# A hybrid encoder layer: the input projection of twelve of seventeen tiles in seven-product form, with the heads' data kept in DRAM and one triangular solve per group

## The chip, the cores and the metric

The kernel runs on one NeuronCore of a Trainium2 chip. The metric is the device time of one execution in microseconds (us). Engines are named as in the profile: PE (TensorE), DVE (VectorE), ACT (ScalarE), POOL (GpSimd), SP (the sync engine, which here only issues transfers).

## The reference

One layer runs over 2048 new prompt frames (16 tiles of 128 rows) and over eight running streams of 16 frames (one more tile, "the sample tile", number 16). Width is 1024, everything is float32.

```
h = rmsnorm(x, norm_mix_pre);  P = h @ w_in        # 1024 -> 3592 columns
q,k,v = silu(causal_dwconv4(P[:, :1536]));  q,k = l2norm per head (4 heads x 128)
beta = sigmoid(b);  g = -exp(a_log) * softplus(a + dt_bias)
S_t = exp(g_t) (I - beta_t k_t k_t^T) S_{t-1} + beta_t k_t v_t^T;  o_t = S_t^T q_t
o = rmsnorm_head(o) * silu(z);  y = B * causal_dwconv3(C * H)
x = x + rmsnorm(concat(o, y) @ w_o)
x = x + rmsnorm((silu(h2 @ w_gate) * (h2 @ w_up)) @ w_down),  h2 = rmsnorm(x)
```

The recurrence is computed tile by tile: a unit lower triangular 128 x 128 matrix per tile and head is inverted, and the state S passes from tile to tile. Outputs are y, the new states and the last rows of both convolutions.

## The kernel before

Every float32 product is split into a rounded part and a remainder (hi and lo, type fp32r) and made from three products: hi·hi, hi·lo, lo·hi. A split is a cast on ACT and a subtraction on DVE or POOL.

The kernel has four stages. The first is what the change touches:

- **First stage.** `GROUPS` holds six groups of three tiles (the last has two). For each group the loop in the body runs, in this order: `x_prep` (row norms, split of the transposed input into eight hi and eight lo tiles), `gate_prep`, `qkv_stage`, `pair_stage`, `level_stage`, `z_stage`, a `chunk_stage` or `sample_stage` for each tile, `sc_stage`.
- `project` (its products are recorded at L136, the helper `mm3`) makes one of 28 column blocks of 128: eight k-slices times three products, 128x128 against the group's 384 (or 256) columns, into one PSUM bank. The bank pool psd has three. `weights` splits a block the first time (L338 cast, L340 subtraction), writes the split form to DRAM (`wsplit`, L343), and later groups load 1 MB back from there (L332). Some blocks are split in every second group or in the last one as well.
- `conv_qkv` does the causal convolution: a copy out of PSUM (L379), a first multiply (L381), three taps (L367), SiLU (L390). Keys are transposed, scaled and transposed back; queries and values are transposed. Results stay in SBUF.
- `pair_stage` makes, for each tile, the matrices k·k and k·q with decay (L491, L492, L495, L496), sends the sixteen 32 x 32 diagonal blocks of each tile to DRAM, gathers them with one block on each partition, and solves all of the group's blocks at once: 31 steps of a product and a subtraction on DVE (L511, L513), 48 partitions for three tiles.
- `level_stage` brings the inverted blocks back and joins them to inverses of 64 and of 128 (L538 to L562); a POOL memset (L552) stands between two of its steps. `chunk_stage` advances the state (L592 to L609) and makes the output (L613 to L619); `out_stage` norms it and writes it to `mixd`.
- **Output projection** (`o_tile`, L758): one tile at a time, reading `mixd`, all 17.
- **Feed-forward, up** (L963) and **down** (L1122) use a seven-product scheme: a 2 x 2 block product is made from seven block products instead of eight, of sums of the weight blocks and of the input blocks, and recombined on ACT, DVE and POOL (L999 to L1014). Sums of the weights are L929 to L932, splits L938 and L939.

The order of instructions on each engine comes from a scheduler that runs through the program in order of a simulated time; earlier program text has the higher priority. Loads are issued by SP, most stores by ACT's queue, each queue in order.

## Time and profile before

| | us |
|---|---|
| runs shown, median (lowest to highest) | 2668.58 (2663.05 to 2671.18) |
| profiled execution, span | 2659.7 |
| PE / DVE / ACT / POOL busy | 2533.2 / 1717.3 / 971.8 / 939.5 |
| first stage, first to last projection product | 22.5 to 991 |
| output projection | 1010 to 1225 |
| feed-forward up | 1225 to 2167 |
| feed-forward down | 2167 to 2660 |

Of the profiled execution only the span is known, the time from its first to its last instruction. Busy times are those of instructions; issuing transfers and waiting on semaphores are not counted. PE's records are pipelined, so neighbouring products overlap in them: the pitch from start to start says what one costs.

### The profile page before, as it was taken

How to read it: one execution, taken by the hardware profiler on the slowest of the kernel's cores; microseconds unless marked ns; L12 is line 12 of the kernel's file. 1: busy time of each engine (PE TensorE's matmuls, PEld its weight loads, DVE VectorE, ACT ScalarE, POOL GpSimd, SP SyncE). 2: the span in 40 equal slices, each digit the busy share in tenths (PEclk: the TensorE clock that was granted, in tenths of full speed). 3: DMA queues.
4: the chain of work that ended last, by engine and by line, in shares of the span. 5: the costliest groups of instructions: out<-in, count | busy, mean ns of one | idle time of the engine just before them, and what ended most of it. 6: DMA issues, size and time to landing. Idle time of an engine off the chain costs nothing.

```text
span 2659.7 us, 42363 instructions
## 1 busy us (share of the span) xinstructions
PE 2533.2 (95%) x15129; PEld 2357.1 (89%) x15129; DVE 1717.3 (65%) x3403; ACT 971.8 (37%) x2337; POOL 939.5 (35%) x841
## 2 busy tenths in 40 slices
PE   7989899999999989999999999999899999999997
PEld 6889789989899987878999999999899987887776
DVE  7788567667575875676978863433633344677698
ACT  5535115142251524433434432222323335333343
POOL 2321001000010210224556654443544445555563
PEclk9999989999999998999999999999999999999999
DMA  6876576666657555667877777877888852443365
GB/s 206 293 255 243 166 245 216 226 225 239 214 207 248 177 182 173 230 214 250 309 261 271 265 259 250 282 247 240 286 287 278 276 169 87 129 123 119 126 217 176
DMA packets 322403, 589.46 MB, mean 222 GB/s; under 512 B 57116, under 2 KB 206304, under 8 KB 303376
## 3 DMA queue, kind: packets, MB, share of 16 engines
q1 hardware_dynamic: 193600, 510.01, 56.7%
q10 hardware_dynamic: 128592, 76.74, 9.5%
q8 instruction: 120, 1.97, 0.3%
q14 instruction: 91, 0.75, 0.1%
HBM read 424.60 MB, written 162.05 MB: 221 GB/s over the span
## 4 chain that ended last, share of the span: by engine, by line
PE 67%; DVE 13%; DMA 8%; issue 4%; ACT 3%; POOL 2%; SPq 1%; ACTq 1%; DVEq 0%; POOLq 0%
PE fbank L963 28%; PE dbank L136 16%; PE fbank L1122 10%; PE tbank L758 3%; PE dbank L758 3%; DMA w<-wsplit 2%; DMA wr<-in_w_in 1%; DVE acc L367 1%; DVE xl L894 1%; POOL dw L829 1%; DMA dr<-in_w_dn 1%; DVE xr L1137 1%; DVE acc L1081 1%; DVE acc L1136 1%; DMA xt<-in_x 1%
## 5 line engine op out<-in xcount | busy, mean ns | idle before, releaser
L963 PE MATMUL fbank<-xh,fw 128*128 128x384 f32 (+1 forms) x3696 | 904.2, 327 | 19.7 <-ACT m L999 12.1
L136 PE MATMUL dbank<-hi,w 128*128 128x384 f32 (+1 forms) x2688 | 691.9, 336 | 16.6 <-DMA w<-wsplit 9.7
L963 PEld LDWEIGHTS fbank<-xh,fw 128*128 128x128 f32 x3696 | 654.9, 189 | 23.4 <-ACT m L999 14.2
L963 PE MATMUL fbank<-xl,fw 128*128 128x384 f32 (+1 forms) x1848 | 604.2, 327 | 0.0
L136 PEld LDWEIGHTS dbank<-hi,w 128*128 128x128 f32 x2688 | 484.8, 193 | 22.8 <-POOL w L340 8.4
L1122 PE MATMUL fbank<-dw,as 128*128 128x512 f32 x1980 | 463.2, 395 | 14.3 <-ACT dw L827 5.0
L1122 PEld LDWEIGHTS fbank<-dw,as 128*128 128x128 f32 x1980 | 372.0, 189 | 105.2 <-DVE acc L1081 7.4
L136 PE MATMUL dbank<-lo,w 128*128 128x384 f32 (+1 forms) x1344 | 449.5, 335 | 0.0
L963 PEld LDWEIGHTS fbank<-xl,fw 128*128 128x128 f32 x1848 | 348.9, 189 | 0.0
L136 PEld LDWEIGHTS dbank<-lo,w 128*128 128x128 f32 x1344 | 259.0, 193 | 1.7 <-issue 0.8
L1106 POOL TENSOR_TENSOR as<-ar,as 128x256 fp32r<-128x256 f32 (+1 forms) x207 | 188.2, 918 | 171.8 <-ACT as L1103 170.4
L939 POOL TENSOR_TENSOR fw<-rg,fw 128x512 fp32r<-128x512 f32 x124 | 176.5, 1424 | 180.9 <-ACT fw L938 180.7
L1081 DVE TENSOR_TENSOR acc<-acc,fbank 128x512 f32<-128x512 f32 x248 | 166.6, 682 | 99.6 <-PE fbank L1122 79.6
L1103 ACT CAST as<-ar 128x256 fp32r<-128x256 f32 (+1 forms) x288 | 118.3, 427 | 181.8 <-PE fbank L1122 132.7
L340 POOL TENSOR_TENSOR w<-wr,w 128x512 fp32r<-128x512 f32 x49 | 78.3, 1599 | 223.6 <-ACT w L338 188.0
L938 ACT CAST fw<-rg 128x512 fp32r<-128x512 f32 x124 | 77.5, 625 | 185.1 <-PE fbank L963 147.9
L367 DVE SCALAR_TENSOR_TENSOR acc<-R,cw,acc 128x384 f32<-128x384 f32 (+1 forms) x216 | 131.0, 609 | 2.0
L1007 DVE TENSOR_TENSOR u<-m,fbank 128x384 f32<-128x384 f32 (+1 forms) x66 | 34.8, 528 | 143.3 <-PE fbank L963 130.4
L1008 POOL TENSOR_TENSOR m<-m,m 128x384 f32<-128x384 f32 (+1 forms) x66 | 69.4, 1051 | 159.5 <-ACT m L1001 119.0
L939 POOL TENSOR_TENSOR fw<-ru,fw 128x512 fp32r<-128x512 f32 x62 | 92.3, 1488 | 85.8 <-ACT fw L938 70.2
L1012 DVE TENSOR_TENSOR c<-u,fbank 128x384 f32<-128x384 f32 (+1 forms) x66 | 34.9, 528 | 127.8 <-PE fbank L963 127.6
L552 POOL MEMSET AU<- 32x128 f32 x16 | 3.2, 197 | 281.0 <-PE gbank L538 272.1
(322 smaller groups left out, 3807.2 us busy)
## 6 DMA issues: line engine op xcount, KB each, us to landing
w<-wsplit SPq DMA_DIRECT2D x119, 1024.0 KB, 6.0
fw<-fsplit SPq DMA_DIRECT2D x188, 512.0 KB, 4.7
fsplit<-fw SPq DMA_DIRECT2D x94, 512.0 KB, 4.1
partd<-pt ACTq DMA_DIRECT2D x88, 384.0 KB, 6.0
rg<-in_w_gu SPq DMA_DIRECT2D x62, 512.0 KB, 3.7
wsplit<-w SPq DMA_DIRECT2D x28, 1024.0 KB, 4.7
wr<-in_w_in SPq DMA_DIRECT2D x98, 256.0 KB, 4.4
ar<-partd SPq DMA_DIRECT2D x48, 384.0 KB, 3.3
```

Of the source, the lines that this page charges most:

```text
L136: T.matmul(ps, l, r, start=(i == 0), stop=(i == n - 1))
L340: e.tensor_tensor(out=wl[:, c], in0=wr, in1=wh[:, c].bitcast(F32), op=ALU.subtract)
L367: V.scalar_tensor_tensor(acc, raw(d), w[:, d:d + 1], acc, op0=ALU.mult, op1=ALU.add)
L758: T.matmul(pss[n], m_[:, j, :], w_[k][:, n * 512:(n + 1) * 512], start=(k == 0 and ci == 0), stop=(k == KD - 1 and ci == 2))
L938: A.copy(w[:, 0], v)
L939: e.tensor_tensor(out=w[:, 1], in0=v, in1=w[:, 0].bitcast(F32), op=ALU.subtract)
L963: T.matmul(ps, w_[:, c], b_[k][:, :hw], start=(first and k == 0 and ci == 0), stop=(k == KH - 1 and ci == 2), skip_group_check=not first)
L1008: G.tensor_tensor(out=s7, in0=s7, in1=s5, op=ALU.add)
L1081: V.tensor_add(dst, dst, ps)
L1103: ins = A.copy(a[:, 0, :n], v)
L1106: e.tensor_tensor(out=a[:, 1, :n], in0=v, in1=a[:, 0, :n].bitcast(F32), op=ALU.subtract)
L1122: T.matmul(ps, a[:, x_, q * P:(q + 1) * P], w[:, y_], start=(start and q == 0 and ci == 0), stop=(q == c - 1 and ci == 2), skip_group_chec ...
```

## The change

The tiles are grouped anew and the groups are taken in pairs, "super-groups" of five, six and six tiles:

```
-GROUPS = [[0, 1, 16], [2, 3, 4], [5, 6, 7], [8, 9, 10], [11, 12, 13], [14, 15]]
+GROUPS = [[0, 1, 16], [2, 3], [4, 5, 6], [7, 8, 9], [10, 11, 12], [13, 14, 15]]
+SUPER = [[0, 1], [2, 3], [4, 5]]
-NPD, NPT, NPG = 3, 2, 2
+NPD, NPT, NPG = 4, 2, 2
+NX, NX0, NW, NWR, NST, NACC = 56, 32, 8, 4, 2, 3
```

The 28 column blocks are taken in 14 pairs, in the order z, k, q, v, z, then the short convolution's blocks. The first super-group projects as before, with the same split weights for both its groups (`plain_unit`); on the way it writes four sums of the weight blocks to DRAM. The two others load blocks and sums, split them anew (seven tiles of 128x512 per pair, eight buffers) and use seven products:

```
+        def plain_weights(p):
+            ...
+            W = [wsplit(r, G if i < 3 else V) for i, r in enumerate(raw)]
+            V.tensor_add(a22, a21, a22)
+            nc.sync.dma_start(out=wsums[p][:, 0], in_=a22)
+            V.tensor_sub(a21, a11, a21)
+            ...
+            G.tensor_tensor(out=a11, in0=a22, in1=a11, op=ALU.subtract)
+            ...
+            V.tensor_sub(a12, a12, a11)
+            ...
+        def product_weights(p):
+            r = []
+            for i, src in enumerate((quad(p, 0), wsums[p][:, 0], wsums[p][:, 1], wsums[p][:, 2],
+                                     quad(p, 1), wsums[p][:, 3], quad(p, 3))):
+                raw = raw_tile()
+                nc.sync.dma_start(out=raw, in_=src)
+                r.append(wsplit(raw, V if i in (2, 5) else G))
+            return r
+        def product(ps, w, b, first):
+            for k in range(KD // 2):
+                c = slice(k * P, (k + 1) * P)
+                for ci, (x_, y_) in enumerate(((0, 0), (0, 1), (1, 0))):
+                    T.matmul(ps, w[:, x_, c], b[k][y_], ...)
+        def paired_unit(si, p):
+            X, W = xops[si], ready.pop((si, p))
+            banks = [dbank()[:, :W1] for _ in range(4)]
+            for i, b in enumerate(banks):
+                product(b, W[i], X[PX[i]], True)
+            b1, b4, b2, b3 = banks
+            s1, s7, s5 = (new("s", W1) for _ in range(3))
+            A.copy(s1, b1)
+            A.copy(s5, b4)
+            A.copy(s7, b3)
+            for b, i in ((b1, 4), (b4, 5), (b3, 6)):
+                product(b, W[i], X[PX[i]], False)
+            ...
+            V.tensor_add(u2, s1, b2)
+            G.tensor_tensor(out=s7, in0=s7, in1=s5, op=ALU.add)
+            ...
+            V.tensor_add(v1[:, h2], u2, b4)
+            V.tensor_add(v2[:, h1], u2, b3)
+            G.tensor_tensor(out=v2[:, h2], in0=s7, in1=u2, op=ALU.add)
```

`x_rows` replaces `x_prep`: it loads the transposed input of a whole super-group, sums squares over its eight slices (ACT squares, DVE adds), gets the column sums from PE, and scales. `x_ops` makes the seven combinations of input blocks and their splits, 28 pairs of tiles; there are 56 such tiles, and both paired super-groups use them. The convolution runs over 768 columns, and its first multiply is now an ACT copy with a scale:

```
+        def conv_rows(ci, R):
+            ...
+            A.activation(acc, R[:, 3:3 + W2], AF.Copy, scale=w[:, 3:4])
+            taps(acc, lambda d: R[:, d:d + W2], w, 4)
+            A.activation(acc, acc, AF.Silu)
```

The heads' data (k transposed and not, q, v, SiLU of z) and both pair matrices of each tile go to DRAM from ACT's queue and are loaded tile by tile (SP) where they are used. The recurrence is a generator, `steps(si)`, advanced between the units by a table: pair tiles at the sixth unit of a super-group, the solve's 31 steps in four parts over the next ones, then levels and chunks.

```
+        def steps(si):
+            ...
+            for t in tiles:
+                pair_tile(t)
+                yield
+            yield from solve_stage(si)
+            level_tile(tiles[0])
+            level_tile(tiles[1])
+            yield
+            for k, t in enumerate(tiles):
+                ...
+                    state_now[0], before, after = chunk_stage(t, state_now[0], oo[k % 2], before, after)
+                ...
+                if k + 2 < len(tiles):
+                    level_tile(tiles[k + 2])
+                yield
+        for si in (1, 2):
+            xops[si] = x_ops(staged)
+            for p in range(NPAIR):
+                if p == 5:
+                    bg.append(steps(si))
+                step(PLAN[si][p])
+                ...
+                paired_unit(si, p)
```

`pair_tile`, `level_tile`, `chunk_stage` and `out_stage` make the same products as before; the diagonal blocks are stored from ACT's queue instead of SP's; the output part of a chunk (`before`, `after`) is issued inside the next tile's chunk. One solve serves a super-group (80 or 96 partitions). `o_tile` takes both of its banks from psd, which has four now.

More of the change, by code (lines that the diff above doesn't have):

```diff
@@ L360, in fetch, with dt_prep @@
-        def fetch():
-            if order:
-                j, gi = order.pop(0)
-                pending.append((j, *weights(j, gi)))
-        def taps(acc, raw, w, n, cols):
+            ssq = gp.tile([P, MAXT, H], F32, name=f"ssq{gi}")
+            return dict(sb=sb, nG=nG, eG=eG, tl=tl, eL=eL, eLs=eLs, grow=grow, ssq=ssq)
+        def dt_prep(t, i, gt, dt):
+            nc.sync.dma_start(out=dt, in_=gt["grow"][4 * i:4 * i + 4].partition_broadcast(P))
+            for h in range(H):
+                V.scalar_tensor_tensor(dt[:, h, :], dt[:, h, :], gt["nG"][:, 4 * i + h:4 * i + h + 1],
+                                       neg_s if t == SAMPLE else neg_p, op0=ALU.add, op1=ALU.add)
+            A.activation(dt, dt, AF.Exp)
@@ new lines, in steps, with step @@
+                if k:
+                    done.append(tiles[k - 1])
+                if k + 2 < len(tiles):
+                    level_tile(tiles[k + 2])
+                yield
+            before()
+            after()
+            done.append(tiles[-1])
+        def step(n=1):
+            for _ in range(n):
+                while bg:
+                    try:
+                        next(bg[0])
+                        break
+                    except StopIteration:
+                        bg.pop(0)
+            return bool(bg)
@@ L785, in o_tile @@
             nc.scalar.dma_start(out=hTd[gi][:, :, i * P:(i + 1) * P], in_=ht)
-        for t in range(O_SPLIT):
+        pft = None
+        otodo = list(range(O_SPLIT))
+        while step():
+            for _ in range(2):
+                if otodo and otodo[0] in done:
+                    o_tile(otodo.pop(0))
+        nc.scalar.dma_start(out=state_p, in_=state_now[0])
+        mid.close()
+        ps_g.close()
+        pft = ps_p.enter_context(tc.tile_pool(name="pft", bufs=8 - NPD - NPT, space=PSUM, reuse_waits="tile"))
+        for t in otodo:
             o_tile(t)
```

851 lines of the change are left out of this document (496 added, 355 removed).

## The prediction

> **What bounds the kernel now.** I read the engine totals first, then the windows of the first stage, then single rows.
>
> ```profile
> span 2659.7 us, 42363 instructions
> PE 2533.2 (95%) x15129; PEld 2357.1 (89%) x15129; DVE 1717.3 (65%) x3403; ACT 971.8 (37%) x2337; POOL 939.5 (35%) x841
> PE 67%; DVE 13%; DMA 8%; issue 4%; ACT 3%; POOL 2%; SPq 1%; ACTq 1%; DVEq 0%; POOLq 0%
> ```
>
> TensorE is busy 95% of the span and carries 67% of the chain that ended last; nothing else comes near. The span is 2659.7 us; the runs shown are 3.4 to 11.5 us longer than it, and their median, 2668.58, is 8.9 us longer. I make the sum against the span and add 8.9.
>
> The change touches only the stage up to the output projection, so the windows are cut at the group borders of that stage (columns: us, then PE, PEld, DVE, ACT, POOL busy, granted clock, DMA share, GB/s).
>
> ```profile
> 22.00:181.00 159.00, 143.65 (x818) 136.88 (x819) 128.70 (x354) 78.65 (x188) 49.90 (x36) 0.98 0.75 259
> 181.00:389.00 208.00, 189.83 (x1321) 175.59 (x1320) 138.95 (x362) 63.08 (x175) 29.73 (x33) 0.93 0.61 209
> 389.00:549.00 160.00, 157.21 (x1146) 151.13 (x1147) 103.82 (x295) 54.04 (x153) 12.42 (x14) 0.99 0.69 234
> 711.00:872.00 161.00, 157.49 (x1121) 152.18 (x1120) 103.86 (x296) 54.16 (x154) 13.74 (x15) 0.98 0.62 214
> 991.00:1010.00 19.00, 8.99 (x135) 7.50 (x135) 6.70 (x15) 4.96 (x10) 0.39 (x2) 0.58 0.57 159
> 1225.00:1560.00 335.00, 326.15 (x1864) 323.02 (x1863) 273.28 (x324) 139.38 (x286) 199.97 (x139) 0.99 0.81 281
> 22.00:1010.00 988.00, 928.41 (x6553) 884.42 (x6554) 684.85 (x1888) 359.26 (x974) 146.70 (x137) 0.96 0.65 221
> ```
>
> A steady group of three tiles takes 160 us and leaves TensorE idle under 2.5%. The first two groups, with VectorE at 81% and 67%, leave it idle 9.7% and 8.7%. In the whole stage (last row, 988 us) TensorE is busy 94%, VectorE 69%, ScalarE 36%, GpSimd 15%. The row 1225 to 1560 is the feed-forward stage, already in seven-product form: VectorE 82%, GpSimd 60%, TensorE still idle only 2.6%.
>
> **Products removed.** A pair of weight blocks against two groups of three tiles costs now 2 x 2 x 24 = 96 products of 384 columns; in seven-product form 7 x 4 x 3 = 84. Twelve tiles go that way: 14 pairs x 12 x 2 = 336 products fewer. The 672 of 256 columns stay, for the two-tile group is only moved. Price of one:
>
> ```profile
> 215.99 0.51 PE L136 MATMUL dbank<-hi,w 128*128 128x384 f32 x2
> 216.34 0.33 PE L136 MATMUL dbank<-lo,w 128*128 128x384 f32 x1
> 216.51 0.51 PE L136 MATMUL dbank<-hi,w 128*128 128x384 f32 x2
> L136 PE MATMUL dbank<-hi,w 128*128 128x384 f32 x2240 | 603.3, 345 | 13.6 <-POOL w L340 6.8 <-DMA w<-wsplit 6.7
> L136 PE MATMUL tbank<-hi,wba 128*16 128x384 f32 x40 | 14.6, 364 | 2.6 <-ACT hi L243 2.6
> ```
>
> Three start in each 0.52 us (215.99 to 216.51), so one costs 0.174 us; its recorded 345 ns overlaps the next one. 336 x 0.174 = **-58 us**. By recorded times it would be 336 x 0.345 = -116 us, which I reject: 3360 such products would fill 1159 us, more than the 988 us of the stage. The gate product gets 16 more narrow products and the column sums that replace the row-wise squares some 14; at the same pitch, with some room for single ones, **+6 us**. Transposes, pair, level and recurrence products keep their number. TensorE's demand of 988 us becomes about 930 at the present idle share.
>
> **VectorE.** Rows of the whole stage and, for the last five rows, of the feed-forward stage from 1225 to 1560:
>
> ```profile
> 22.00:1010.00 988.00, 68.78 (x186) 0.96 0.65 221
> 22.00:1010.00 988.00, 62.90 (x186) 0.96 0.65 221
> L381 DVE TENSOR_SCALAR acc<-R,cw 128x384 f32<-128x384 f32 x48 | 19.8, 413 | 0.0
> L381 DVE TENSOR_SCALAR acc<-R,cw 128x256 f32<-128x256 f32 x24 | 8.3, 347 | 4.1 <-ACT vraw L390 3.9
> L367 DVE SCALAR_TENSOR_TENSOR acc<-R,cw,acc 128x384 f32<-128x384 f32 x144 | 92.4, 644 | 1.8
> L340 DVE TENSOR_TENSOR w<-wr,w 128x512 fp32r<-128x512 f32 x49 | 35.7, 729 | 11.5 <-ACT w L338 10.6 <-POOL w L340 0.9
> L932 DVE TENSOR_TENSOR sD<-rg,sB 128x512 f32<-128x512 f32 x21 | 29.1, 1386 | 0.6
> L931 DVE TENSOR_TENSOR sB<-sA,rg 128x512 f32<-128x512 f32 x20 | 14.7, 737 | 0.0
> L1007 DVE TENSOR_TENSOR u<-m,fbank 128x384 f32<-128x384 f32 x22 | 11.9, 543 | 0.0
> L939 POOL TENSOR_TENSOR fw<-rg,fw 128x512 fp32r<-128x512 f32 x43 | 70.7, 1645 | 21.4 <-ACT fw L938 21.2
> L1008 POOL TENSOR_TENSOR m<-m,m 128x384 f32<-128x384 f32 x22 | 27.5, 1248 | 47.7 <-issue 33.6 <-ACT m L1001 11.3 <-DVE pt L1035 2.8
> ```
>
> The first two rows are the solve's two lines (L511, L513): 132 us for six solves; three go, since one for five or six tiles issues the same 62 instructions: -66. The first multiply of each convolution (L381: 28 us, with the short convolution's some 36) moves to ScalarE: -36. Weight work: 49 subtractions become 14 x 4 (one subtraction, three sums) and 28 x 2, so 63 more at 0.73: +46. Recombining the products: 3 additions from PSUM in 28 units at 0.54: +46. Taps over 768 columns instead of twice 384 save fixed cost, the sums over the inputs cost some: together I estimate 0, from -25 to +25. So 685 - 66 - 36 + 46 + 46 = 675 us.
>
> But GpSimd is no longer empty. Weight subtractions and sums there go from 49 to 196 (147 x 1.6 = 235), recombination brings 56 at 1.25 (70), input subtractions some 36 at 1.25 (45): from 147 to about 500 us of 930, 54%. In the feed-forward stage, where it is at 60%, VectorE work between two SBUF operands swells: the same 512-column form is 0.73 us in the first stage and 0.74 to 1.39 there (L931, L932), with a middle of 1.06, x1.45; work that reads PSUM does not (L1007, 0.54). Some 400 of the 675 us is of the first kind (taps 150 after the rows of L367, weights 82, solve 66, inputs and recurrence an estimated 100): 400 x 0.45 x 54/60 = +162, so **VectorE about 835 of 930 us, 90%**. Bounds: 675 with no collision, and 400 x 0.90 x 54/60 = +324, so 1000, if all swell as L932 does.
>
> The Trainium skill (SBUF — State Buffer, section "SBUF: two separate sides") says that GpSimd and a VectorE instruction with two SBUF inputs hold one port pair as an exclusive lock, and that the other "fully blocks". The trace agrees in kind (L932 doubled, L1007 untouched). If every one of the 350 us added on GpSimd blocked VectorE, it would need 675 + 350 = 1025 us and would bound the stage; with +162 it does not.
>
> **ScalarE and the queues.**
>
> ```profile
> L338 ACT CAST w<-wr 128x512 fp32r<-128x512 f32 x98 | 58.0, 620 | 70.1 <-DMA wr<-in_w_in 35.1 <-PE dbank L136 22.4 <-DMA mixd<-yo 5.1
> L379 ACT COPY R<-dbank 128x384 f32<-128x384 f32 x48 | 22.6, 473 | 15.6 <-PE dbank L136 15.5
> L479 ACTq DMA_DIRECT2D mixd<-yo x68: 326/442/1552, 137.7 to 991.9; - x68
> mixd<-ot ACTq DMA_DIRECT2D x17, 256.0 KB, 2.6
> dt<-grow SPq DMA_DIRECT2D x17, 256.0 KB, 4.4
> w<-wsplit SPq DMA_DIRECT2D x119, 1024.0 KB, 6.0
> wr<-in_w_in SPq DMA_DIRECT2D x98, 256.0 KB, 4.4
> ```
>
> ScalarE gains 252 - 98 = 154 casts (+95), 84 copies out of PSUM (+40), the moved multiplies (+36), input casts (some +20): 359 becomes 550. Its queue also issues about 320 transfers instead of 110 (heads' k, v, q, z; the diagonal blocks, which leave SP; the two pair results): at 0.44 us each 140 us, so about 690 of 930, 74%. No bound, but each store sits in front of a copy that frees a product bank.
>
> Bytes fall: weights were 119 + 28 transfers of 1 MB and 98 of 0.25 (172 MB); now 56 + 56 + 196 of 0.25 (77 MB) plus the heads' data, 7 x 17 written and 9 x 17 read at 0.25 (68 MB). Each head tile makes a trip through DRAM, 2.6 to 6.0 us to write and 4 to 6 to read, behind other loads on SP. It is hidden behind nine units of 84 products (15 us each), and in the last super-group behind output tiles. With the cover gone, a level step waits as now at 991 to 1010, 10 us idle in 19; six tiles instead of two could expose up to 30 us. I take no change there, since output tiles 0 to 9 are ready.
>
> New waits and what is queued behind them: a head load that waits on SP for its buffer or for the store before it holds up the weight loads behind, and TensorE, with eight split weight tiles for the seven of a unit, waits for those. On GpSimd the memset in the level step waits for TensorE:
>
> ```profile
> L552 POOL MEMSET AU<- 32x128 f32 x16 | 3.2, 197 | 281.0 <-PE gbank L538 272.1
> ```
>
> Those 272 us cost nothing while GpSimd is empty; now weight subtractions stand behind each of the 16. And the third super-group reuses all 56 input slots of the second, so its first four splits (a cast as L379, a subtraction as L1008) may be late once, 0 to 6 us. All of this is priced in the next part.
>
> **Friction, the unknown term.** All three helpers go from 69, 36 and 15% to about 90, 74 and 54%, with in-order queues and four product banks, all used by each unit; the next unit's first product waits until bank one is copied out behind taps. The nearest rows: with helpers this loaded the feed-forward stage idles TensorE 2.6%, the first group 9.7%. Today's steady groups idle 2.3%, so the added friction lies between 0 and 7.4% of 930 us, 0 to +69. Feed-forward units have eight banks and no solve, the first group has a start-up: I go a third of the way, 2.6%, **+24 us**.
>
> **Sum.** 2659.7 - 58 + 6 + 24 = 2632 us of span, 2640 as a median (-1.1%).
>
> **Rivals.**
> - *Full gain.* The helpers stay hidden as in the feed-forward stage: friction 0, 2608 span, 2617. For it: that stage's 2.6%. Against: 90% on VectorE.
> - *Nothing left.* Friction of 45 to 60 us eats the gain: 2653 to 2668 span, 2662 to 2677.
> - *VectorE becomes the bound.* Each two-SBUF-operand instruction pays what L932 pays: VectorE needs 1000 us, at the 97% that TensorE reaches 1031, against 988 today: 2703 span, 2711, slower. It decides once VectorE's need passes 0.97 x 988 = 958, that is once collisions cost over 283 us. For it: L932, and 90% already by my own sum. Against: L931 beside it in the same code at 0.74. By the Trainium skill's lock (SBUF — State Buffer, "SBUF: two separate sides") at its hardest, 1025 / 0.97 = 1057, it would be 2737; L931 shows that not every instruction is caught.
> - *Banks.* A unit's first product waits behind two 768-column taps (about 1 us each by L367) and one recombination, 3 us in each of 28 units: +84 instead of +24, 2692 span, 2701. Against it, the feed-forward stage with eight banks:
>
> ```profile
> PE fbank L963 <- ACT m L999: 12.1, 7, 3.7
> ```
>
> 12 us in 66 units.
>
> **How the numbers follow.** Chances: full gain 0.25, forecast 0.37, nothing left 0.14, VectorE bound 0.16, banks 0.08. About 0.3%, 8 us, is what the runs can tell from no change; the first two are faster (0.62), the third the same (0.14), the last two slower (0.24). The range, 2605 to 2712, leaves out what lies beyond full gain (fewer waits for solves) and a VectorE above 1000 us or a long tail; the forecast's own range is 2622 to 2656.
>
> **What would show it.** Right: 3024 products of 384 columns at 0.17 to 0.18 us pitch and 672 of 256; the output projection starting near 980 instead of 1010; VectorE 85 to 92% of the stage; the two-SBUF forms between 0.9 and 1.4 us per 512 columns; 186 solve rows down to 93 in each line. Wrong: the chain of waits showing VectorE taps or recombination more often than products in the first stage, product waits on ScalarE or VectorE above 60 us, or more than 30 us of idle TensorE before the first output tile.

## The result, and the profile after

The changed kernel takes 2781.88 us (median; 2775.86 to 2783.16), the kernel before on the same chip 2669.88: a ratio of 1.042 (95% interval 1.040 to 1.044). The forecast of 2640 missed by 142 us, and it missed the sign. The profiled execution:

```profile
span 2780.3 us, 42995 instructions
PE 2535.2 (91%) x14837; PEld 2340.5 (84%) x14837; DVE 1818.9 (65%) x3034; ACT 1119.8 (40%) x2608; POOL 1273.5 (46%) x1080
PE 47%; DVE 11%; DMA 6%; issue 3%; POOL 2%; ACT 1%; ACTq 1%; SPq 0%; DVEq 0%; POOLq 0%
```

TensorE is as busy as before in microseconds (2535 against 2533) although it issues fewer products; its share of the chain that ended last fell from 67% to 47%. The windows at the new stage borders (us, then PE, PEld, DVE, ACT, POOL busy, granted clock, DMA share, GB/s):

```profile
22.00:1062.00 1040.00, 894.72 (x5950) 837.16 (x5951) 773.15 (x1471) 494.94 (x1205) 474.98 (x360) 0.93 0.57 169
28.00:337.00 309.00, 263.09 (x1721) 250.49 (x1722) 233.02 (x544) 139.44 (x359) 113.72 (x85) 0.93 0.56 173
337.00:702.00 365.00, 312.77 (x1946) 290.54 (x1945) 273.60 (x457) 179.71 (x423) 192.91 (x141) 0.92 0.56 164
702.00:1038.00 336.00, 300.40 (x2103) 280.55 (x2102) 248.46 (x443) 168.85 (x407) 163.70 (x131) 0.96 0.58 169
1038.00:1062.00 24.00, 16.73 (x184) 15.00 (x184) 12.10 (x23) 5.72 (x15) 1.17 (x2) 0.85 0.70 211
1062.00:1183.00 121.00, 100.36 (x653) 83.35 (x653) 64.67 (x134) 36.58 (x104) 15.40 (x20) 0.88 0.51 164
1183.00:1339.00 156.00, 146.82 (x673) 121.65 (x673) 102.91 (x197) 60.27 (x152) 35.58 (x41) 0.96 0.64 212
```

Row one is the whole first stage: VectorE is busy 74% of it, ScalarE 48%, GpSimd 46%. No engine is full, and TensorE still idles 14%, more than any stage of the kernel before. Rows three and four are the second and third super-groups, in seven-product form: 365 and 336 us for six tiles, where the kernel before needs 322 in plain form (389 to 711). The last two rows are the stretch up to the feed-forward stage: 277 us of output projection instead of 215, the first 121 of it at a clock of 0.88 and TensorE 17% idle.

So the 114 us by which the feed-forward stage starts later (1339 instead of 1225) are 47 at the last projection product (1038 instead of 991) and 67 behind it; the feed-forward stages give 7 more.

### The profile page after: what moved, and what is told of

The parts are those of the page before. It is cut to its first block, busy times and chain, and to the rows that moved or that the text cites. A ratio compares the mean times of both kernels' runs of the same rounds, so it can differ in the third digit from the quotient of the medians.

```text
span 2780.3 us, 42995 instructions
## 1 busy us (share of the span) xinstructions
PE 2535.2 (91%) x14837; PEld 2340.5 (84%) x14837; DVE 1818.9 (65%) x3034; ACT 1119.8 (40%) x2608; POOL 1273.5 (46%) x1080
## 4 chain that ended last, share of the span: by engine, by line
PE 47%; DVE 11%; DMA 6%; issue 3%; POOL 2%; ACT 1%; ACTq 1%; SPq 0%; DVEq 0%; POOLq 0%
PE fbank L1231 28%; PE fbank L1390 10%; PE dbank L1016 5%; PE dbank L577 2%; DVE xl L1162 1%; POOL dw L1097 1%; DMA fh<-hTd 1%; DMA hTd<-ht 1%; DMA dr<-in_w_dn 1%; DVE xr L1405 1%; DVE acc L442 1%; DVE Ts L702 1%; DVE pr L700 1%; DVE acc L1404 1%; DVE acc L1349 1%
## 5 line engine op out<-in xcount | busy, mean ns | idle before, releaser
L577 PE MATMUL dbank<-xh,w 128*128 128x384 f32 x1568 | 438.1, 355 | 40.5 <-ACT s L588 12.0
L392 POOL TENSOR_TENSOR w<-wr,w 128x512 fp32r<-128x512 f32 x182 | 276.3, 1527 | 288.3 <-ACT w L391 278.2
L577 PEld LDWEIGHTS dbank<-xh,w 128*128 128x128 f32 x1568 | 298.4, 198 | 49.0 <-ACT s L588 12.9
L577 PE MATMUL dbank<-xl,w 128*128 128x384 f32 x784 | 276.0, 352 | 2.7 <-DVE xl L216 2.6
L391 ACT CAST w<-wr 128x512 fp32r<-128x512 f32 x252 | 153.1, 618 | 192.2 <-PE dbank L577 61.5
L147 PE MATMUL dbank<-xh,w 128*128 128x384 f32 (+1 forms) x896 | 214.4, 327 | 17.4 <-ACT Rs L459 10.2
L147 PEld LDWEIGHTS dbank<-xh,w 128*128 128x128 f32 x896 | 161.0, 201 | 21.9 <-ACT Rs L459 11.0
L577 PEld LDWEIGHTS dbank<-xl,w 128*128 128x128 f32 x784 | 155.7, 199 | 5.2 <-DVE xl L216 3.2
L147 PE MATMUL dbank<-xl,w 128*128 128x384 f32 (+1 forms) x448 | 145.6, 326 | 4.1 <-DVE xl L216 2.3
L442 DVE SCALAR_TENSOR_TENSOR acc<-R,cw,acc 128x256 f32<-128x256 f32 (+1 forms) x144 | 125.9, 877 | 31.1 <-ACT acc L454 23.4
```

The costliest lines, as they stand in the source:

```text
L147: T.matmul(ps, l, r, start=(i == 0), stop=(i == n - 1))
L391: A.copy(w[:, 0], v)
L392: e.tensor_tensor(out=w[:, 1], in0=v, in1=w[:, 0].bitcast(F32), op=ALU.subtract)
L442: V.scalar_tensor_tensor(acc, raw(d), w[:, d:d + 1], acc, op0=ALU.mult, op1=ALU.add)
L577: T.matmul(ps, w[:, x_, c], b[k][y_], start=(first and k == 0 and ci == 0), stop=(k == KD // 2 - 1 and ci == 2), skip_group_check=not first)
```

## The experiments

Each is the changed kernel with one edit, unless it says otherwise, and each ratio is to the kernel before on the same chip. The table has what its trace shows: the end of the first super-group and of all projection products, the first pair product of the third super-group, the last chunk's state product, and the start of the feed-forward stage. Each edit also changes the order that the scheduler finds: in e1, e10, e11, e12 and e14 the program of the first super-group is that of the changed kernel, and it ends at 335 to 339, so differences of two or three us in this table say nothing.

| run | ratio (95%) | first group ends | products end | third pair tiles | last chunk | feed-forward |
|---|---|---|---|---|---|---|
| changed kernel | 1.042 (1.040-1.044) | 337 | 1038 | 893 | 1157 | 1339 |
| e1_tail | 1.037 (1.034-1.039) | 335 | 1037 | 890 | 1163 | 1318 |
| e2_nosolve | 1.022 (1.020-1.025) | 349 | 1032 | 860 | 1089 | 1294 |
| e3_pairstores_sp | 1.034 (1.032-1.036) | 334 | 1018 | 871 | 1133 | 1319 |
| e4_keep_split | 1.052 (1.050-1.054) | 335 | 1029 | 939 | 1183 | 1364 |
| e5_plain | 1.010 (1.008-1.012) | 318 | 996 | 803 | 1051 | 1252 |
| e6_banks | 1.056 (1.053-1.058) | 359 | 1080 | 912 | 1199 | 1371 |
| e7_split_once | 1.047 (1.045-1.049) | 360 | 1030 | 927 | 1170 | 1350 |
| e8_split_once_tail_sp | 1.029 (1.027-1.031) | 369 | 1027 | 916 | 1209 | 1308 |
| e9_plain_tail_sp | 1.005 (1.003-1.007) | 319 | 996 | 800 | 1035 | 1247 |
| e10_bank_order | 1.039 (1.037-1.041) | 335 | 1034 | 888 | 1149 | 1331 |
| e11_no_taps | 1.031 (1.028-1.033) | 339 | 1021 | 857 | 1125 | 1307 |
| e12_seven_in_one | 1.033 (1.030-1.035) | 337 | 1039 | 875 | 1123 | 1316 |
| e13_all_stores_sp | 1.038 (1.035-1.040) | 342 | 1030 | 874 | 1146 | 1331 |
| e14_no_recurrence_2 | 1.030 (1.028-1.032) | 335 | 1016 | 847 | 1129 | 1313 |
| e15_no_splits | 1.025 (1.023-1.027) | 334 | 973 | 868 | 1120 | 1303 |
| e16_plain_keep | 1.001 (1.000-1.002) | 311 | 980 | 791 | 1032 | 1233 |
| e17_kv4 | 1.041 (1.039-1.043) | 335 | 1037 | 893 | 1152 | 1333 |
| e18_plain_buffers | **0.993 (0.991-0.995)** | 290 | 956 | 769 | 1011 | 1208 |

### First round: four suspects

**The output tiles' transposes in other banks.**

```
-                ps = bank() if pft is None else pft.tile([P, 512], F32, tag="t", name="ftbank")
+                ps = tbank()
```

> The output tiles' transposes use the two PSUM banks of pool pst, which the projection no longer needs by then, instead of banks that come free only with the last step of the recurrence. Nothing else changes. Tail theory (the output stage is long because its transposes must wait for the recurrence's two banks): the first output transposes start within 15 us of the first output product instead of 110 us after it, output products run through, the output stage falls from 277 to 215-235 us, the time from 2782 to 2722-2745. Rival (the tail is long because the recurrence itself takes DVE, ACT and the loads' queue, and output tiles only fill what is left): under 15 us, 2767-2782.

A gain of 0.6% of the time (some 16 us): between the two, not the 40 to 60 of the tail theory. Two rows of the changed kernel show the mechanism (first and last start are the numbers behind the durations), the third is the edit's:

```profile
L792 PE MATMUL gbank<-S,kTl x48: 275/377/580, 1040.3 to 1157.1; 128*128 128x128 f32 x48
L1039 PE MATMUL ftbank<-cst,hx x136: 270/273/474, 1172.1 to 1349.8; 128*128 128x128 f32 x136
L1039 PE MATMUL tbank<-cst,hx x136: 269/273/447, 1110.0 to 1328.4; 128*128 128x128 f32 x136
```

The first transposition of an output tile comes 15 us behind the last chunk, since the banks of `pft` are those of the recurrence. With free banks it comes at 1110, and the output tiles run during the recurrence, but each then takes 14 to 17 us instead of 12.

**No solve.**

```
             for j in range(31):
                 ...
+                continue
                 pr = wk.tile([P, 512], F32, tag="kl", name="pr")
```

> Leaves out the 31 steps of all three triangular solves (its loads, stores and everything round it stay; the inverses are then the identity's). Local VectorE bound theory (VectorE is busy 93% and 97% in the two stretches of the solve under the seven-product units, 602-684 and 958-1010, and TensorE loses there): 62 steps x 3 go, some 135 us of VectorE, and first-stage TensorE idle falls by 25-45 us; also the recurrence of the last group starts 48 us earlier and the tail shrinks by 20-40: 2782 to 2700-2735. Rival (coupling by queues, banks and few buffers, not VectorE's time): the first stage shrinks under 12 us, and only the tail gains: 2745-2765.

```profile
602.00:684.00 82.00, 68.89 (x358) 66.30 (x357) 76.32 (x124) 33.51 (x65) 58.26 (x34) 0.92 0.33 98
958.00:1010.00 52.00, 44.33 (x248) 42.43 (x246) 50.63 (x89) 17.24 (x32) 29.37 (x21) 1.00 0.41 121
```

These two rows of the changed kernel were the reason for the theory: VectorE 93% and 97% busy. Without the solves the products end only 6 us earlier; most of the gain (1.9%) lies behind them, the last chunk coming 68 us earlier. The total is that of the first theory, its place is mostly the rival's. Mostly, because the first super-group ends 12 us later here (349, not explained), so that the two paired ones take 683 us instead of 701: a locally full VectorE cost the units up to 18 us, less than the 25 to 45 of the theory.

**Pair stores from SP.**

```
-                nc.scalar.dma_start(out=sad[si]...)          # and aud, qkd
+                nc.sync.dma_start(out=sad[si]...)
```

> The 102 stores of the pair tiles (diagonal blocks and both pair matrices) are issued by SP instead of by ACT's queue. Theory that stores on ACT's in-order queue hold up copies out of product banks and casts: ACT's waits behind those stores (39 us on three lines) go, the first stage shrinks by 12-30 us: 2752-2770. Rival (ACT has slack, and the weight loads behind the stores on SP are late instead): 2778-2795.

Held: products end 20 us earlier, and everything behind comes 20 to 24 us earlier.

**Splits kept from the second super-group for the third.**

```
+            if si == 2:
+                ... nc.sync.dma_start(out=r[-1].bitcast(F32), in_=wkeep[p][:, i])
...
+                nc.sync.dma_start(out=wkeep[p][:, i], in_=r[-1].bitcast(F32))
```

> The second super-group writes its split weights to DRAM, the third loads them split: 98 casts and 98 subtractions fewer (some 60 us of ACT, 120 us of GpSimd, 25 us of VectorE, and what these collide with), 75 MB of transfers more. Re-splitting theory: the units of the third super-group run as with free helpers, its stretch 702-1038 falls from 336 to 305-320 us: 2752-2768. Rival (transfers: DMA share is 0.74-0.87 in parts of it; or splits were hidden): 2778-2800, the second super-group longer for its stores.

Both were half right: the third super-group's units fall from 336 to 300 us, the second's, which writes 49 MB, rise from 365 to 394, and the pair tiles come 46 us later. In all 0.9% slower.

### Second round: the form itself, the banks, the splits

**Plain form.** Groups, DRAM, one solve and the interleaving stay; only the projection of twelve tiles is plain again.

```
-                paired_unit(si, p)
+                for s_ in range(2):
+                    for q_ in range(2):
+                        plain_unit(p, q_, s_, si)
```

> The second and third super-group project in plain form, as the first does: 4 x 24 products of 384 columns per pair instead of 84, four weight splits per pair instead of seven, no sums, no recombination, convolutions over 384 columns. Groups, data through DRAM, one solve per super-group and the interleaved recurrence stay. Theory that the seven-product form's own helper work (splits, recombination, few buffers) eats its 58 us: the stage gets no longer than before by more than 10 us, 2760-2792. Rival (the form pays its 58 us and the loss comes from the regrouped recurrence and its trips): 2815-2845.

Below the lowest time that either gave: 2694, 3.1% less than the changed kernel. The seven-product form, which removes 58 us of products, costs 87 net on this skeleton; the skeleton alone (new groups, trips through DRAM, three solves, interleaving) costs 1.0%.

```profile
318.00:664.00 346.00, 328.90 (x2323) 311.71 (x2321) 224.87 (x502) 162.89 (x405) 101.21 (x86) 0.98 0.52 155
664.00:996.00 332.00, 321.75 (x2324) 306.27 (x2323) 193.10 (x460) 148.92 (x374) 73.19 (x65) 0.99 0.48 140
996.00:1018.00 22.00, 12.60 (x128) 10.83 (x126) 10.92 (x22) 5.96 (x16) 2.43 (x4) 0.68 0.85 260
1018.00:1252.00 234.00, 218.62 (x1084) 181.99 (x1085) 148.97 (x287) 89.62 (x228) 44.70 (x52) 0.96 0.61 200
```

Its second and third super-groups, with more products, take 346 and 332 us against 365 and 336, at 95 and 97% of TensorE. Of the 87 us, 19 lie in the first super-group (318 against 337; the sums of the weights and their stores are what differs, apart from work fetched ahead for the second), 23 in the other two, 45 between the last product and the feed-forward stage.

**Five product banks, one for transposes.**

```
-NPD, NPT, NPG = 4, 2, 2
+NPD, NPT, NPG = 5, 1, 2
```

> Five product banks and one bank for transposes and gates instead of four and two. Banks theory (a unit's first product waits for the copy out of bank one of the unit before): product waits on ACT's copies and on the recombination's additions (some 33 us) fall by half or more and with them half-clock stretches: 2735-2765. Rival (banks are not what the products wait for; the transposes now wait on their one bank): 2776-2800.

1.3% slower than the changed kernel: what a fifth product bank gives is not seen, since the second transposition bank is worth more. The clean test of the banks is e10.

**Splits made once, in the first super-group.**

```
+            for v, j, e in ((a22, 1, G), (a21, 3, V), (a11, 2, G), (a12, 5, G)):
+                w = wf.tile([P, 2, 512], F32R, tag="ws", name="ws", bufs=2)
+                ... cast, subtraction, nc.sync.dma_start(out=wkeep[p][:, j], ...)
```

> All seven split tiles of each weight pair are made once, in the first super-group (56 casts and 56 subtractions more there), and kept in DRAM; the two others load them split (196 casts, 140 subtractions on GpSimd and 56 on VectorE fewer there). Transfers: 49 MB written instead of 14 in the first super-group, 98 MB read instead of 49 in the others. Re-splitting theory (keeping the splits for the third alone took its units from 336 to 300 us, and the gain was given back by stores under the second and a late recurrence): second plus third super-group 701 to 620-650 us, the first 309 to 320-335: 2715-2755 in all. Rival (what is saved there comes back as waits for transfers or as a later recurrence, as before): 2772-2800.

The rival held: the two paired super-groups fall from 701 to 670 us, the first grows by 23, and the pair tiles are 34 us later still. One stall of this trace shows how a queue holds TensorE up. The timeline of ScalarE (start, length, what), then of TensorE, around 981 us:

```profile
975.35 6.09 ACTq L525 DMA_DIRECT2D mixd<-acc  x6
981.55 0.63 ACT L385 ACTIVATE dt<-dt 128x512 f32<-128x512 f32 x1 [14.80 <-DMA mixd<-acc]
981.57 1.39 ACTq L525 DMA_DIRECT2D mixd<-acc  x3
983.78 3.79 ACTq L683 DMA_DIRECT2D sad<-AU  x4
...
989.55 2.44 ACTq L525 DMA_DIRECT2D mixd<-acc  x3
992.09 0.48 ACT L590 COPY s<-dbank 128x384 f32<-128x384 f32 x1 [9.91 <-issue]
```

```profile
980.93 0.34 PE L579 MATMUL dbank<-xh,w 128*128 128x384 f32 x1
992.62 0.69 PE L579 MATMUL dbank<-xh,w 128*128 128x384 f32 x1 [11.35 <-ACT s L590]
993.10 0.52 PE L579 MATMUL dbank<-xl,w 128*128 128x384 f32 x1
```

ScalarE is hardly busy in this stretch, by the busy count: it issues stores in program order, and the copy that frees the product bank stands behind them. A merged line holds the pauses between its stores too. Three of the stores by themselves:

```profile
975.97 1.33 ACTq L525 DMA_DIRECT2D mixd<-acc  x1
983.78 0.36 ACTq L683 DMA_DIRECT2D sad<-AU  x1
986.28 0.33 ACTq L683 DMA_DIRECT2D sad<-AU  x1
```

A store takes 0.3 to 1.3 us here, and between two of them up to 2.1 us pass (984.14 to 986.28) in which the second waits for a semaphore; by the semaphore's updates, for an earlier transfer to land. So the queue holds the copy up by both, the issuing and the waits between, 5.5 us of the 9.9 being issuing. TensorE waits 11.35 us and then starts its products first 0.48, then 0.32 us apart instead of 0.174, at a granted clock of 0.50:

```profile
992.60:996.00 3.40, 3.38 (x11) 3.38 (x12) 0.63 (x2) 0.73 (x2) 2.00 (x2) 0.50 0.64 204
```

The Trainium skill (TensorE: Matmul & The Clock Gate, section "What's actually happening") has the array at half rate after an idle window; this clock and these starts agree.

**The three repairs together** (e7, e1, e3).

> The three together: splits made once, output transposes in the free banks, pair stores from SP. If the three causes are separate, their gains add (about 20 and 17 us for the last two): 2680-2720. If they are one queue of helper work seen from three sides, the sum is under two thirds of that: 2725-2750. Against the kernel before (2668) a gain is expected by neither.

The second expectation's time, 1.3% under the changed kernel, but not its reason: e7 is no gain, and the three separate ratios multiply to 1.033, so the edits add up, and a little more.

### Third round

**Plain form with both cheap repairs** (e5, e1, e3).

> The plain form in all three super-groups (2694) with the two cheap repairs: pair stores from SP, output transposes in the free banks. If both causes are at work under the plain form too, 12-25 us go: 2668-2683, level with the kernel before at best. If they hurt only because the seven-product units left ACT and VectorE no slack, under 8 us: 2687-2697.

2684, at the border of the two: they are worth 0.4% there against 1.4% under the seven-product form.

**Another order of the product banks.**

```
-            banks = [dbank()[:, :W1] for _ in range(4)]
+            banks = [dbank(i)[:, :W1] for i in border[0]]
+            border[0] = [border[0][i] for i in (2, 0, 1, 3)]
```

> The changed kernel, with the four product banks handed out in another order from unit to unit: the next unit starts in the bank that the unit before finished longest ago (the one with a single group of products), so that each bank has at least 6.3 us to be read out instead of 4.2 (groups of 12 products at 0.174 us; the shortest time from the end of a bank's last group to the next unit's first group in it). No work is added or removed. Drain theory (product waits on s, R and acc, and the half clock after each, come from banks not yet read): 15-40 us less, 2740-2767. Rival (helpers are late by more than 6 us when they are late, or for other reasons): 2774-2790.

0.3% (intervals 1.037-1.041 and 1.040-1.044), products 4 us earlier, the rival's size: half as much time again to read each bank buys almost nothing. That a reader, when it is late, is late by more is the reading that this leaves.

**No taps in the seven-product units.**

```
-            taps(acc, lambda d: R[:, d:d + W2], w, 4)
+            pass
```

> Leaves out the three taps of the convolutions of q, k and v in the seven-product units (72 VectorE instructions of some 1.2 us, 85 us of VectorE); everything else stays. Drain theory and VectorE theory both expect the reads of the banks, which stand behind these taps, to come earlier: 30-60 us less, 2720-2752. If neither holds (units late for weights, transfers or queues): under 12 us, 2768-2785.

1.1% less, the least that the theories gave: 85 us of VectorE taken away end the products 17 us earlier.

**Seven products in the second super-group only.**

```
             for p in range(NPAIR):
                 ...
+                if si == 1:
+                    paired_unit(si, p)
+                    continue
+                ... four plain_unit
```

> Seven-product form in the second super-group only, the third in plain form. Tail theory (of what the form costs, about half is that the last group's heads are ready late, in bursts, so that its recurrence runs 94 us past the last product instead of 19): the stretch from the last projection product to the feed-forward stage falls from 301 to 250-262 us: 2722-2742. Rival (the form costs by the unit, wherever it stands: half of the 87 us): 2738-2750 with the tail unchanged in size and the third stretch shorter.

2759, above both. The stretch behind the products falls from 301 to 277, about half of what the tail theory gave. The third stretch, plain, is no shorter (339 us), and its pair tiles start at 875, 33 us behind the last stored q of its heads (842), because the second super-group's last chunk is only at 848; e14 takes that up.

### Fourth round: what was still open

**All first-stage stores from SP.**

```
-            nc.scalar.dma_start(out=ktd[gi][:, h], ...)     # and kTd, qTd, vtd, szd, mixd, the pair stores
+            nc.sync.dma_start(out=ktd[gi][:, h], ...)
```

> As the run that moved the pair stores to SP, with the heads' stores (k twice, q, v, SiLU of z: 120) and the short convolution's 68 moved too. Store-queue theory (each store on ACT's queue stands in front of copies that free product banks): a further 10-20 us beyond the 22 of the pair stores, 2738-2750. Rival (only the pair stores come in bursts long enough to matter, and SP's queue now holds loads behind stores that wait for data): 2752-2785.

The rival's time: no better than moving the pair stores alone, if anything worse (1.035-1.040 against 1.032-1.036). Whether only the bursts mattered, or what ScalarE's queue won was lost on SP's, this run does not tell apart.

**No recurrence in the second super-group.**

```
+            if si == 1:
+                for t in tiles: ... # one load, one store
+                return
```

> Leaves out the levels, the chunks and the outputs of the second super-group's recurrence (its pair tiles and its solve stay; one load and one store per tile stand in). Chain theory (pair tiles, solve, levels and chunks of one super-group share single buffers with those of the next, so under the seven-product units, where one takes some 360 us, the next one's pair tiles start when it ends and not when their heads are there): the third super-group's pair tiles start at most 25 us after its sixth unit starts instead of 53, its recurrence ends at most 65 us after the last product instead of 120, and the stretch from the last product to the feed-forward stage falls from 301 to 255-275 us; with the lighter third stretch 2690-2735 in all. Rival (the pair tiles are late for their heads, which come in bursts): they start 45 us or more after the sixth unit, and the stretch stays above 285: 2740-2765.

Mixed, and the chain theory did not carry: the pair tiles start 35 us (the second of them 58) after the sixth unit, and the stretch stays 297 us. The heads are now the late ones. Rows of the key stores of the third super-group (`kTd`; first to last start), in the changed kernel, with one more buffer (e17), without the second recurrence, and in plain form:

```profile
L498 ACTq DMA_DIRECT2D kTd<-kv x8: 326/326/354, 792.6 to 871.7; - x8
```

```profile
L498 ACTq DMA_DIRECT2D kTd<-kv x8: 326/326/397, 791.5 to 869.9; - x8
```

```profile
L498 ACTq DMA_DIRECT2D kTd<-kv x8: 326/338/356, 787.2 to 852.2; - x8
```

```profile
L500 ACTq DMA_DIRECT2D kTd<-kv x8: 326/327/338, 724.1 to 780.4; - x8
```

The last key unit ends at 795, 794, 779 and 749: the last key is stored 76, 76, 73 and 31 us behind its unit. In the changed kernel two things hold the pair tiles, the heads (last q stored at 885) and the recurrence before (last chunk at 858, output behind it), and each covers the other; e12 shows the recurrence alone, e14 the heads. The run without splits (e15, next) shows the recurrence once more: there the last q is stored at 815, the last chunk is at 840, and the pair tiles start at 868.

**No splits.**

```
-                r.append(wsplit(raw, V if i in (2, 5) else G))
+                r.append(wtile())
+                nc.sync.dma_start(out=r[-1].bitcast(F32), in_=wone)
```

> Prices the second and third super-groups' weight splits alone: their 196 casts and 196 subtractions are left out, and all their weight tiles are loaded from one split tile kept in DRAM, so the products use wrong weights; the same 512 KB tiles are loaded as where the splits were made once, without the stores and the 56 added splits under the first super-group. Re-splitting theory: second plus third 701 to 640-665 us, the tail 10-30 shorter, 2695-2742. Rival (the units are late for other work, or the 49 MB more of loads take the gain): 2755-2785.

```profile
334.00:652.00 318.00, 294.38 (x1898) 277.20 (x1897) 201.43 (x412) 130.49 (x329) 80.33 (x68) 0.95 0.82 268
652.00:973.00 321.00, 295.08 (x2073) 279.01 (x2071) 188.32 (x409) 111.92 (x304) 66.93 (x66) 0.95 0.78 251
```

Held for the units: 639 us instead of 701. The expected shorter tail did not come, for the pair tiles now start behind the recurrence before and not behind their heads: the stretch behind the products grew from 301 to 330, and only 37 of the 66 us won at the last product reach the feed-forward stage, as many as the last chunk came earlier. What the splits do to VectorE, grouped by shape, 337 to 1038 us, in the changed kernel and without them:

```profile
L442 DVE SCALAR_TENSOR_TENSOR acc<-R,cw,acc 128x768 f32<-128x768 f32 x72 | 84.8, 1181 | 7.4 <-ACT acc L472 7.1
L392 DVE TENSOR_TENSOR w<-wr,w 128x512 fp32r<-128x512 f32 x55 | 47.9, 871 | 24.9 <-ACT w L391 24.9
L491 DVE TENSOR_TENSOR rkr<-rkr,sb 128x3 f32<-128x3 f32 x16 | 15.7, 983 | 5.2 <-POOL rkr L141 5.0
L599 DVE TENSOR_TENSOR s<-s,dbank 128x384 f32<-128x384 f32 x28 | 15.2, 544 | 7.9 <-PE dbank L577 7.8
```

```profile
L444 DVE SCALAR_TENSOR_TENSOR acc<-R,cw,acc 128x768 f32<-128x768 f32 x72 | 72.8, 1013 | 21.9 <-ACT acc L474 21.3
L493 DVE TENSOR_TENSOR rkr<-rkr,sb 128x3 f32<-128x3 f32 x16 | 3.6, 225 | 5.0 <-POOL rkr L142 4.9
L601 DVE TENSOR_TENSOR s<-s,dbank 128x384 f32<-128x384 f32 x28 | 15.3, 547 | 15.5 <-ACT s L590 13.3 <-PE dbank L579 2.2
```

With 140 subtractions fewer on GpSimd (and 56 fewer on VectorE, 196 casts fewer on ScalarE), a tap falls from 1.18 to 1.01 us, the key's scale of three columns from 0.98 to 0.23, and the addition that reads PSUM stays at 0.54. The Trainium skill (SBUF — State Buffer, section "SBUF: two separate sides") has the shared port pair as an exclusive lock, held for a whole instruction: the three-column row, which does next to no work and still takes 0.76 us longer, agrees.

**Plain form, splits kept, both repairs; then with more buffers.**

```
+            for i in range(4):
+                nc.sync.dma_start(out=wkeep[p][:, i], in_=W[i].bitcast(F32))     # first group; the others load it
```

> Plain form throughout with both cheap repairs (2684), and the first super-group's split weights kept in DRAM for the two others (112 casts and 112 subtractions fewer, 28 MB more written, 56 MB more read). If splits cost by helper time: 8-20 us less, 2664-2676, level with the kernel before. If the plain units already hide them: 2678-2695.

```
-  {"R": 2, "acc": NACC, "s": 3, "kv": 3}          # R and acc 768 columns wide
+  {"R": 4, "acc": 6, "s": 3, "kv": 6}             # R and acc 384 columns wide, NX 53
```

> The plain version with kept splits and both repairs (2674, level with the kernel before), with its convolution buffers cut to the 384 columns that it uses and doubled in number (R 2 to 4, acc 3 to 6) and six kv buffers instead of three. If few buffers still hold its units or heads up: 4-14 us less, 2660-2670, faster than the kernel before by 0-0.4%. If not: 2671-2678.

Kept splits: the first expectation held, level with the kernel before (1.000 to 1.002). This is also the closest comparison of the two forms: with splits made once and both repairs the seven-product form stands at 1.029 (e8), the plain form at 1.001. The buffers gave 26 us, more than the 4 to 14 expected: 2648, 0.7% under the kernel before (0.991 to 0.995) and 4.7% under the changed one by the two ratios; the best version of this study. Its windows, one for each super-group:

```profile
22.00:290.00 268.00, 238.35 (x1578) 229.23 (x1579) 181.12 (x482) 138.46 (x349) 76.67 (x57) 0.94 0.73 246
290.00:624.00 334.00, 331.59 (x2366) 315.35 (x2365) 201.74 (x494) 136.03 (x350) 36.80 (x46) 0.99 0.66 203
624.00:956.00 332.00, 327.76 (x2442) 312.16 (x2440) 173.80 (x464) 124.20 (x334) 25.66 (x31) 1.00 0.62 190
```

TensorE idles 1% in the last two. Most of the gain lies in the first super-group (290 against 311 us).

**One more kv buffer in the changed kernel.**

```
-{"R": 2, "acc": NACC, "s": 3, "kv": 3}
+{"R": 2, "acc": NACC, "s": 3, "kv": 4}
```

> The changed kernel with four instead of three buffers for the heads' transposed and scaled tiles (kv; 1.5 KB per partition, all that is free). Buffer theory (in the third super-group the eight key stores follow one another every 10.8 us, from 789 to 872, 77 us after the unit that made the last of them, because two such buffers serve each head and come free only when its stores have landed): the spacing falls to about 8 us, pair tiles start at most 35 us after the sixth unit starts instead of 52, 10-25 us less in all: 2757-2772. Rival (the heads wait for their turn on ACT and VectorE among casts, taps and recombination): spacing and time as they are, 2774-2790.

No difference (1.039-1.043 against 1.040-1.044), and the key stores keep their spacing, as the second of the four rows above shows: the heads do not wait for this buffer. That they wait for their turn in the order of ACT, VectorE and PE is what is left, not shown by itself.

## Why the prediction was wrong, step by step

**Products, right.** The page has 1568 + 784 + 448 + 224 = 3024 of 384 columns and 672 of 256, and the median distance from start to start is still 0.174 us. The mean distance to the next start on TensorE, of whatever kind, is 0.219 in the paired units (514.6 us over 2352 products), where the kernel before has 0.190: 105 us above the median's pace (before: 54, over 3360), about 60 in 28 gaps of over a microsecond and the rest in slow stretches. The products were saved and the time was not.

**Helper loads, right in size.** VectorE 773 us of the window where I said 835, GpSimd 475 for 500, ScalarE 495 for 550. The swelling that I took from the feed-forward stage is there too, but smaller: the weight subtraction of 512 columns goes from 0.73 to 0.87 us (L392), x1.2 and not x1.45, and 773 is 98 above the 675 without collisions, not 162. VectorE is 74% busy and not 90, so the rival in which it becomes the bound did not happen either: the stage is 52 us longer without it.

**Friction, the step that failed first.** I took +24 us, at most +69, from the idle shares of stages "with helpers this loaded". By my sum the products should have ended at 991 - 58 + 6 + 24 = 963; they ended at 1038, so the term measured +99. Runs show what is in it: 19 us for the sums of the weights in the first super-group, which I had as VectorE time and at nothing on the path (e5); some 62 us for re-splitting seven tiles per pair (e15); pair stores on ACT's queue 20 (e3); taps 17 (e11); solves 6 at the last product, 18 in the paired super-groups (e2); bank order 4, hardly more than the order's own scatter (e10). They overlap and are not to be added. Moving the splits did not help this form: kept in DRAM (e4, e7), they gave back under one super-group and behind the products what they saved under another. An idle share says how much work helpers have, not how late the one instruction is on which a bank, a weight tile or a head hangs. Here all the helpers' work stands in fixed order in front of it, and each of the pieces left out (sums, splits, taps, solves) gave something, whether its engine was full or not.

**The tail, the step that failed second.** I took no change, "since output tiles 0 to 9 are ready". The stretch behind the last product grew by 67 us. The tiles were ready and could not run through: the transposes' banks were the recurrence's until its end, which is worth some 16 us (e1). The rest goes with the late recurrence. In the changed kernel and in the nine runs that keep its third super-group, its solve and its banks for the transposes (e3, e4, e7, e10, e11, e13, e14, e15, e17), the feed-forward stage starts 180 to 187 us behind the last chunk, at chunk times from 1120 to 1183: that chunk sets the end. Six tiles need 243 to 282 us from the first pair product to it in those runs, and the pair tiles start 52 us after the sixth unit (892.7 against 840.5) for the two reasons that cover each other. I bounded this by two exposed tiles of the kernel before; it was a chain of six with its start late. Friction 75 us above my term, the tail 67 and the feed-forward stages 7 make up the whole miss of the span (2780 against 2632).

**Banks rival.** Its sign was right, and its path is there, but it is not the bulk: products of the paired units wait 43 us on ScalarE and VectorE by the profile (source view of L577), another bank order gave 8 us (e10), the taps gone 17 at the last product (e11). No run removed the wait for a bank altogether.

**Signs.** The output projection started at 1062, not 980, which was the clear one; VectorE at 74% was outside its 85 to 92 as well. Of the three that I named for "wrong", one fired, narrowly: the projection's products wait 64 us on ScalarE and VectorE in the first stage (43 in the paired units, 21 in the first super-group), and I had named 60. The chain cut to this stage still has the paired products (5.5% of the span) ahead of the taps (1.6%), and TensorE is busy 17 of the 24 us ahead of the first output tile. Direct waits undercount the loss, for the slow clock behind each wait is not in them (granted clock 0.92 and 0.96 in the paired super-groups).

**Open.** How much of the 62 us of the splits is VectorE's collision with GpSimd, how much the chain load, cast, subtraction, product through eight weight tiles for seven, and how much ScalarE's 196 casts, was not separated. Nor was it tried whether more R, acc and kv buffers, which together gave the plain form 26 us, would give the seven-product form its gain: its 56 input tiles leave no room for them.

## What to carry to other kernels

Price a scheme that saves products by the work that it puts in front of the instructions that free banks, weight tiles and inputs for the next stage, not by the helpers' busy shares: here a 45 to 75% load was enough to lose 3%. Before putting buffers into a scheme, try the same skeleton without it: plain products with kept splits, the two repairs and small, plentiful buffers beat both kernels. Where a lagging chain and the next stage share banks, the end of the chain sets the end, and gains ahead of it that do not move the chain vanish: 29 of the 66 us in e15.

## What the runs showed of the hardware that was not expected

- A VectorE product of three columns took 0.98 us on average beside GpSimd's subtractions and 0.23 without most of them, while a tap of 768 columns took 1.18 and 1.01: the small instruction between two SBUF operands lost more than the large one.
- A run of stores on ScalarE's queue held one bank's copy for 9.9 us without any of that in the profile's busy count: twelve stores of 0.3 to 1.1 us each, and between them waits of up to 2.1 us, which end, by the semaphores, when earlier transfers land.
- Giving one of two transposition banks to the products cost 1.3% on balance (e6).
